# Silu in place of Sigmoid, and one product less on VectorE, in the experts of a mixture-of-experts layer on one Trainium2 core

## The chip, the cores and the metric

The kernel runs on one core of one Trainium2 chip. The metric is the time of one execution on the device in microseconds, taken over several runs; the number compared is the median. One further execution was recorded by the hardware profiler, and all rows below come from it. Engine names in rows: PE is TensorE's matmuls, PEld its weight loads, DVE is VectorE, ACT is ScalarE, POOL is GpSimd, SP is SyncE, which issues most DMA transfers here.

## The reference

One layer of a diffusion backbone over 1024 tokens of width 1024: windowed attention and a long convolution, merged and normalised, and then a mixture of 32 experts of which each token uses four. The change lies in the experts alone:

```python
hb = x_pad[tok] @ w1[e] + b1[e]
glu, lin = jnp.split(hb.astype(jnp.float32), 2, axis=-1)
glu = jnp.minimum(glu, SWIGLU_LIMIT)                      # 7.0
lin = jnp.clip(lin, -SWIGLU_LIMIT, SWIGLU_LIMIT)
act = (glu * jax.nn.sigmoid(SWIGLU_ALPHA * glu) * (lin + 1.0)).astype(h.dtype)   # alpha 1.702
yb = (act @ w2[e] + b2[e]).astype(jnp.float32)
```

With silu(z) = z·sigmoid(z), glu·sigmoid(1.702·glu) is silu(1.702·glu)/1.702.

## The kernel before

The first thousand microseconds are the attention, the convolution, the merge and the router. From about 1044 us to 2400 us the 32 experts run, and the last 50 us are the final normalisation.

**Experts.** Each expert has a fixed capacity of token rows (416 for the fullest, down to 32). Two experts are in work at any time, one in lane 0 (the large ones, fullest first) and one in lane 1 (the small ones, emptiest first); a planned list says which lane takes its next step. An expert has eight steps: four of gate and linear columns (two weight blocks each) and four of the output (one block each). A weight block of 1 MB comes from memory by an SP transfer into one of five `raw` buffers (L304). ScalarE rounds it to half precision, `wh` (L314, a Copy with a scale), and VectorE makes the remainder, `wl` (L316); both go in two halves, so that there are 768 of each. When VectorE has made `wl`, the `raw` buffer is free and SP can start the next transfer. TensorE then multiplies in three passes, high by high, high by low and low by high (L346; the smallest experts, of up to 56 rows, L343).

**The gated activation.** For each pair of gate and linear blocks VectorE adds the bias and clamps both from PSUM into SBUF (L392 `sg` and L393 `sl`; for the smallest experts L390 and L395), ScalarE computes the sigmoid of `sg` into `ss` (L396), VectorE multiplies `sg` by `ss` (L397) and then clamps `sl` from below and multiplies it by that product (L398). ScalarE rounds the result to half precision (`ah`, L402) and VectorE makes the remainder (`al`, L403). `ss` has one buffer for each lane, `sg` and `sl` two. `gpool` is false, so that the product runs on VectorE. The values are carried times 64, and L402 and L403 scale them back by 2^-8.

**Tokens in and out.** For each chunk of up to 128 rows of an expert to come, a matmul with a one-hot matrix `S` gives the row numbers (L261, cast to the index `gi` in L263), a GpSimd gather fetches the rows (`g`, L276), TensorE transposes them (L285) and ScalarE copies them to `xT` (L286). At an expert's end TensorE transposes the output, ScalarE scales it into `yr` (L435, two buffers) and a GpSimd scatter-add writes it to memory (`accD`, L436). Gathers and scatter-adds share GpSimd's one queue, in program order.

**Order.** The code is written step by step, but a scheduler that simulates the program's time line places the instructions of each engine. An edit of one operation can therefore move others.

Of the kernel before, what the change touches and what calls it, by code (L numbers as in the profile page):

```python
# [18 lines left out]
AF = mybir.ActivationFunctionType  # L19
ALU = mybir.AluOpType  # L20
# [51 lines left out]
def pecost(C): return (0.192*(mmc(2*C)+mmc(C)) if C<=CCAT else 0.576*mmc(C))+2.0*-(-C//128)  # L72
def dmacost(C): return DMAC+2.1*-(-C//128)
def plan():


    k=sum(map(dmacost,CAPS))/sum(map(pecost,CAPS))
    Q=[r for r in range(NE) if r not in HOLD]; H=list(HOLD); cur=[None,None]; out=[]; pe=PE0; dma=0.0; last=None
    while True:
        for l in range(2):  # L80
            if cur[l] is None and Q and (l==0 or CAPS[Q[-1]]<=LMAX): cur[l]=(Q.pop(0 if l==0 else -1),0)
            elif cur[l] is None and l==1 and H and (len(Q)<=HQ): cur[l]=(H.pop(0),0)
        if cur[0] is None and cur[1] is None: return out
        l=0 if pe<=dma+SLACK else 1
        if cur[l] is not None and last==l and cur[l][1]==4: l=1-l
        if cur[l] is None: l=1-l
        r,u=cur[l]; f=1/6. if u<4 else 1/12.
        pe+=pecost(CAPS[r])*k*f; dma+=dmacost(CAPS[r])*f
        out.append((l,r,u)); last=l
        cur[l]=(r,u+1) if u<7 else None  # L90
PLAN=plan()
PMAX=[max(CAPS[r] for l,r,u in PLAN if l==k) for k in range(2)]
assert sorted((r,u) for l,r,u in PLAN)==[(r,u) for r in range(NE) for u in range(8)]
class Moe:
# [144 lines left out]
    def prep_(s,C,p,pos,M,res,G0=None,late=None):  # L239
# [6 lines left out]
        def hot(i):  # L246
            c0=i*128; cs=min(128,C-c0)
            if late is not None and i>1:
                if i==2: st['w']=wk.tile([128,2,D],F16,name="g1",bufs=2).rearrange("p a (t c) -> p (a t) c",t=4)
                S=st['w'][:,:,(i-2)*128:(i-2)*128+cs]  # L250
            else: S=wk.tile([128,NT,128],F16,name="S%d"%p,bufs=min(2,-(-PMAX[p]//128)))[:,:,:cs]
            st[i]=S
# [25 lines left out]
        def tr(i):  # L278

            if i==0:  # L280
                st['x']=wk.tile([128,2,8,PMAX[p]],F16,name="xT%d"%p,bufs=1); res.append((st['x'],chunks))
            c0=i*128; cs=min(128,C-c0); g=G.pop(i)
# [73 lines left out]
    def expert_(s,C,p,reg,xT,chunks):  # L356
        nc,wk,ps,A=s.nc,s.wk,s.ps,s.A
        e=reg()
        T=lambda dt,name,bufs: wk.tile([128,PMAX[p]],dt,name=name+str(p),bufs=bufs)[:,:C]
        br=s.brs.pop(reg,None)  # L360
        if br is None: br=s.bias_load(e)
        pb=ps.tile([128,512],F32,name="tp",bufs=2)[:,:24]
        nc.tensor.transpose(pb,br,s.idf[:24,:24])
        bc=wk.tile([128,24],F32,name="bc",bufs=4)
        nc.vector.tensor_scalar(bc[:,0:8],pb[:,0:8],64.0,None,op0=ALU.mult)
        nc.vector.tensor_scalar(bc[:,8:16],pb[:,8:16],64.0,64.0,op0=ALU.mult,op1=ALU.add)
        nc.vector.tensor_tensor(bc[:,16:24],pb[:,16:24],s.g2c,op=ALU.mult)
        cat=C<=CCAT
        x=[xT[:,:,k,:C] for k in range(8)] if cat else [[xT[:,q,k,:C] for k in range(8)] for q in range(2)]
        ah,al=[],[]  # L370
        for u in range(4):

            wg=s.jget(); wl=s.jget()
            nb=2 if C<=256 else 1
            for c0 in range(0,2,nb):
                if cat:
                    t=ps.tile([128,4,2,64],F32,name="acc",bufs=4); pg,pl=t[:,0:2,:,:C],t[:,2:4,:,:C]
                elif C<=128:
                    t=ps.tile([128,4,128],F32,name="acc",bufs=4); pg,pl=t[:,0:2,:C],t[:,2:4,:C]
                else:  # L380
                    pg=ps.tile([128,nb,512//nb],F32,name="acc",bufs=4)[:,:,:C]; pl=ps.tile([128,nb,512//nb],F32,name="acc",bufs=4)[:,:,:C]
                for j in range(nb): s.mm3(pg[:,j],wg,c0+j,x,C)
                for j in range(nb): s.mm3(pl[:,j],wl,c0+j,x,C)
                if c0+nb==2: s.jahead(s.ahead)
                T2=lambda dt,name,bufs: wk.tile([128,max(2*PMAX[p],4*CCAT) if PMAX[p]<=256 else 512],dt,name=name+str(p),bufs=bufs)[:,:nb*C].rearrange("p (j c) -> p j c",j=nb)
                g=T2(F32,"sg",2); l=T2(F32,"sl",2); sg=T2(F32,"ss",1)
                for j in range(nb):
                    f=u*2+c0+j
                    if cat:
                        nc.vector.tensor_scalar(g[:,j],pg[:,j,0],bc[:,f:f+1],None,op0=ALU.add); nc.vector.tensor_scalar(l[:,j],pl[:,j,0],bc[:,8+f:9+f],None,op0=ALU.add)  # L390
                        continue
                    nc.vector.tensor_scalar(g[:,j],pg[:,j],bc[:,f:f+1],448.0,op0=ALU.add,op1=ALU.min)  # L392
                    nc.vector.tensor_scalar(l[:,j],pl[:,j],bc[:,8+f:9+f],512.0,op0=ALU.add,op1=ALU.min)  # L393
                if cat:
                    nc.vector.tensor_tensor(g,g,pg[:,:,1],op=ALU.add); nc.vector.tensor_scalar(g,g,448.0,None,op0=ALU.min); nc.vector.tensor_tensor(l,l,pl[:,:,1],op=ALU.add); nc.vector.tensor_scalar(l,l,512.0,None,op0=ALU.min)  # L395
                nc.scalar.activation(sg,g,AF.Sigmoid,scale=1.702/64)  # L396
                (nc.gpsimd if s.gpool else nc.vector).tensor_tensor(g,g,sg,op=ALU.mult)  # L397
                nc.vector.scalar_tensor_tensor(l,l,-384.0,g,op0=ALU.max,op1=ALU.mult)  # L398
                if cat:
                    hl=wk.tile([128,max(2*min(PMAX[p],256),4*CCAT)],F16,name="ah%d"%p,bufs=s.nact(p,nb))[:,:4*C].rearrange("p (j q c) -> p j q c",j=2,q=2); h,lo=hl[:,:,0],hl[:,:,1]  # L400
                else: h=T2(F16,"ah",s.nact(p,nb)); lo=T2(F16,"al",s.nact(p,nb))
                nc.scalar.activation(h,l,AF.Copy,scale=2.**-8)  # L402
                nc.vector.scalar_tensor_tensor(lo,l,2.**-8,h,op0=ALU.mult,op1=ALU.subtract)  # L403
                for j in range(nb):
                    if cat: ah.append(hl[:,j])
                    else: ah.append(h[:,j]); al.append(lo[:,j])
            yield
        yT=[]
        for u in range(4):

            w=s.jget()
            for c in range(2):
                m=u*2+c
                py=ps.tile([128,512],F32,name="acc",bufs=4)
                py=py[:,:2*C].rearrange("p (q c) -> p q c",q=2) if cat else py[:,:C]
                s.mm3(py,w,c,ah if cat else (ah,al),C)
                if c==1: s.jahead(s.ahead)
                y=T(F32,"yT",8)
                if cat:
                    nc.vector.tensor_copy(y,py[:,0]); nc.vector.tensor_tensor(y,y,py[:,1],op=ALU.add); py=y  # L420
                nc.scalar.activation(y,py,AF.Identity,bias=bc[:,16+m:17+m],scale=s.g2s[:,m:m+1])  # L421
                yT.append(y)
            yield
        s.tail.append(s.rows_out(C,chunks,yT))
        yield
# [12 lines left out]
    def experts(s,only=None):  # L438
        P=PLAN[:only]
        s.regs={}; W={}; J=[]  # L440
# [928 lines left out]
```

## Time and profile before

| | |
|---|---|
| time, median of 3 runs | 2435.37 us (2434.03 to 2435.98) |
| the profiled execution's own time | 2453.07 us |
| its span, first to last instruction | 2451.2 us |
| mean granted TensorE clock | 0.936 of full speed |
| TensorE matmuls busy | 2210.8 us, 90% of the span |
| VectorE busy | 2100.5 us, 86% |
| ScalarE busy | 1402.3 us, 57% |
| GpSimd busy | 281.9 us, 12% |

The profiled execution took 17.7 us (0.7%) longer than the median of the runs; stretches and durations are read from it, and the forecast is made for the median. Shares of busy time are means over stages with different limits, so that the experts' stage has to be read by itself.

### The profile page before, as it was taken

To read this page: it belongs to the slowest core of one execution; us is meant where nothing else is said; L and a number is where in the kernel's file an instruction comes from. 1 tells how busy PE (TensorE), PEld (TensorE's weight loads), DVE (VectorE), ACT (ScalarE), POOL (GpSimd) and SP (SyncE) were. 2 spreads that over 40 slices of the span, in tenths; PEclk is the share of its full clock that TensorE was granted. 3 is DMA by queue.
4 is the path that set the end of the run, shared out by engine and by line. 5 is a ranking of instruction groups with operands and counts; after the bars stand their busy time and mean duration, and the time that the engine had idled before them with its cause. 6 is when DMAs were issued, how large, how long until landed. Compare 5 with 4: busy or idle time off the path is not lost.

```text
span 2451.2 us, 59715 instructions
## 1 busy us (share of the span) xinstructions
PE 2210.8 (90%) x24732; PEld 1669.0 (68%) x24753; DVE 2100.5 (86%) x3907; ACT 1402.3 (57%) x2069; POOL 281.9 (12%) x176
## 2 busy tenths in 40 slices
PE   6899989999899999398998999998989999999991
PEld 4565464554544444355566678898989999999991
DVE  6767899798769759789889988998989999999995
ACT  3422334221345412457767767787867878788881
POOL 0000011000000000001021111321041111221110
PEclk9899999999779999689898989999989999999996
DMA  8425644554414332479899989999999999999984
GB/s 287 136 93 181 198 136 138 161 184 159 94 38 148 100 118 104 167 254 304 303 293 313 308 272 339 319 340 325 343 320 348 337 349 335 357 351 353 350 284 157
DMA packets 520012, 594.18 MB, mean 242 GB/s; under 512 B 16708, under 2 KB 472332, under 8 KB 519350
## 3 DMA queue, kind: packets, MB, share of 16 engines
q1 hardware_dynamic: 493048, 508.27, 61.8%
q0 software_dynamic: 13152, 43.69, 6.9%
q10 hardware_dynamic: 13534, 38.35, 4.6%
q8 instruction: 196, 3.21, 0.5%
q14 instruction: 82, 0.67, 0.1%
HBM read 532.95 MB, written 57.29 MB: 241 GB/s over the span
## 4 chain that ended last, share of the span: by engine, by line
PE 59%; DVE 23%; DMA 7%; issue 5%; ACT 3%; SPq 2%; POOL 0%; DVEq 0%; ACTq 0%; POOLq 0%
PE acc L346 30%; PE mm L812 8%; DVE wl L316 8%; PE mm L1080 3%; PE mm L1121 3%; DVE bf L722 3%; PE ff L704 2%; PE acc L343 2%; DMA g<-rows,gi 1%; PE mm L975 1%; DMA accD<-yr,si 1%; ACT wh L314 1%; PE yt L433 1%; PE ff L899 1%; DVE sl L393 1%
## 5 line engine op out<-in xcount | busy, mean ns | idle before, releaser
L316 DVE SCALAR_TENSOR_TENSOR wl<-raw,wh 128x1024 f16<-128x1024 f32 x768 | 910.2, 1216 | 62.1 <-ACT wh L314 59.0
L314 ACT ACTIVATE wh<-raw 128x1024 f16<-128x1024 f32 x768 | 768.1, 1049 | 185.9 <-PE acc L346 80.7
L346 PEld LDWEIGHTS <-wh 128*128 128x128 f16 x9984 | 785.8, 99 | 97.5 <-issue 21.8
L346 PE MATMUL acc<-xT,wh 128*128 128x80 f16 (+18 forms) x6656 | 716.9, 235 | 4.8 <-DVE yT L420 2.2
L346 PE MATMUL acc<-xT,wl 128*128 128x112 f16 (+19 forms) x3328 | 638.0, 235 | 0.0
L346 PEld LDWEIGHTS <-wl 128*128 128x128 f16 x4992 | 493.0, 99 | 46.6 <-issue 10.5
L346 PE MATMUL acc<-ah,wh 128*128 128x112 f16 (+19 forms) x1664 | 331.1, 239 | 14.7 <-ACT ah L402 6.8
L346 PE MATMUL acc<-al,wh 128*128 128x112 f16 (+19 forms) x1664 | 331.9, 240 | 6.6 <-DVE al L403 6.5
L346 PE MATMUL acc<-ah,wl 128*128 128x112 f16 (+19 forms) x1664 | 331.4, 240 | 0.0
L812 PE MATMUL mm<-hx,wh 128*128 128x512 f16 (+1 forms) x1072 | 322.4, 378 | 6.2 <-DVE hx L635 4.6
L812 PE MATMUL mm<-hx,wl 128*128 128x512 f16 x536 | 202.6, 378 | 0.0
L436 POOL DMA_INDIRECT accD<-yr,si x49 | 125.3, 2557 | 668.3 <-ACT yr L435 437.6
L812 PEld LDWEIGHTS <-wh 128*128 128x128 f16 x1072 | 105.0, 98 | 118.4 <-issue 2.3
L276 POOL DMA_INDIRECT g<-rows,gi x44 | 124.2, 2823 | 459.0 <-DVE tf L265 415.6
L722 DVE TENSOR_TENSOR bf<-bf 128x256 f32<-128x256 f32 (+1 forms) x272 | 131.2, 541 | 0.3
L421 ACT ACTIVATE yT<-acc,bc,g2s 128x112 f32<-128x112 f32 (+19 forms) x208 | 97.7, 481 | 28.2 <-PE acc L346 25.6
L812 PEld LDWEIGHTS <-wl 128*128 128x128 f16 x536 | 52.4, 98 | 65.2 <-issue 7.0
L402 ACT ACTIVATE ah<-sl 128x64 f16<-128x64 f32 (+18 forms) x140 | 56.6, 409 | 55.9 <-DVE sl L398 55.6
L343 PEld LDWEIGHTS <-wl 128*128 128x128 f16 x1152 | 79.4, 99 | 12.6 <-issue 11.2
L343 PEld LDWEIGHTS <-wh 128*128 128x128 f16 x1152 | 81.2, 104 | 6.9 <-DVE yT L420 5.2
L393 DVE TENSOR_SCALAR sl<-acc,bc 128x112 f32<-128x112 f32 (+19 forms) x208 | 75.2, 377 | 11.2 <-PE acc L346 10.8
L392 DVE TENSOR_SCALAR sg<-acc,bc 128x112 f32<-128x112 f32 (+19 forms) x208 | 75.3, 378 | 9.2 <-PE acc L346 8.6
(380 smaller groups left out, 3436.1 us busy)
## 6 DMA issues: line engine op xcount, KB each, us to landing
raw<-in_exp_w SPq DMA_DIRECT2D x384, 1024.0 KB
wr<-in_w_in SPq DMA_DIRECT2D x34, 512.0 KB
t<-in_w_mod ACTq DMA_DIRECT2D x32, 512.0 KB
bf<-in_dec SPq DMA_DIRECT2D x32, 256.0 KB
Hd<-bf ACTq DMA_DIRECT2D x32, 256.0 KB
bf<-Hd SPq DMA_DIRECT2D x32, 256.0 KB
Gd<-t ACTq DMA_DIRECT2D x16, 512.0 KB
gt<-Gd SPq DMA_DIRECT2D x32, 256.0 KB
```

The lines of the kernel that those rows point to most:

```text
L276: nc.gpsimd.indirect_dma_start(out=g[:cs].rearrange("p a d -> p (a d)"),out_offset=None,in_=s.rows,in_offset=bass.IndirectOffsetOnAxis(ap= ...
L314: else: nc.scalar.activation(wh[:,o],raw[:,o],AF.Copy,scale=sc)
L316: else: nc.vector.scalar_tensor_tensor(wl[:,o],raw[:,o],64.0,wh[:,o],op0=ALU.mult,op1=ALU.subtract)
L343: nc.tensor.matmul(ps_,wh,x[k],start=k==0,stop=False); nc.tensor.matmul(ps_[:,0],wl,x[k][:,0],start=False,stop=k==7)
L346: nc.tensor.matmul(ps_,a,b,start=n==0,stop=n==23); n+=1
L392: nc.vector.tensor_scalar(g[:,j],pg[:,j],bc[:,f:f+1],448.0,op0=ALU.add,op1=ALU.min)
L393: nc.vector.tensor_scalar(l[:,j],pl[:,j],bc[:,8+f:9+f],512.0,op0=ALU.add,op1=ALU.min)
L421: nc.scalar.activation(y,py,AF.Identity,bias=bc[:,16+m:17+m],scale=s.g2s[:,m:m+1])
L436: st=nc.gpsimd.indirect_dma_start(out=s.accD,out_offset=bass.IndirectOffsetOnAxis(ap=si[:cs,:1],axis=0),in_=yr[:cs],in_offset=None,compute ...
L722: (nc.gpsimd if pool and s.usepool else nc.vector).tensor_tensor(o,a,b,op=op)
L812: nc.tensor.matmul(p,w[a][:,k,:],s.hx[b][:,k,o],start=i==0,stop=i==23); i+=1
L1080: nc.tensor.matmul(p,w[a_][:,k,m*128:(m+1)*128],X[x][:,k,o] if b==0 else X[x][:,k,:],start=n==0,stop=n==11); n+=1
```

## The change

ScalarE's activation is Silu instead of Sigmoid, of the same input with the same scale 1.702/64 into the same buffer `ss`. The product L397 is gone, and the clamp-and-multiply reads `ss` instead of `sg`. Since silu(1.702·glu) is 1.702 times what the product gave, divided by 64, the scale of the two last instructions becomes 0.25/1.702 in place of 2^-8.

```diff
 PLAN=plan()
+HSC=0.25/1.702
...
-                nc.scalar.activation(sg,g,AF.Sigmoid,scale=1.702/64)
-                (nc.gpsimd if s.gpool else nc.vector).tensor_tensor(g,g,sg,op=ALU.mult)
-                nc.vector.scalar_tensor_tensor(l,l,-384.0,g,op0=ALU.max,op1=ALU.mult)
+                nc.scalar.activation(sg,g,AF.Silu,scale=1.702/64)
+                nc.vector.scalar_tensor_tensor(l,l,-384.0,sg,op0=ALU.max,op1=ALU.mult)
...
-                nc.scalar.activation(h,l,AF.Copy,scale=2.**-8)
-                nc.vector.scalar_tensor_tensor(lo,l,2.**-8,h,op0=ALU.mult,op1=ALU.subtract)
+                nc.scalar.activation(h,l,AF.Copy,scale=HSC)
+                nc.vector.scalar_tensor_tensor(lo,l,HSC,h,op0=ALU.mult,op1=ALU.subtract)
```

In the code the Python names `g`, `l` and `sg` stand for the tiles `sg`, `sl` and `ss`. One line is added at the top, so that lines 92 to 396 of the kernel before are 93 to 397 in the changed one; from L398 on the numbers agree again.

On VectorE, the first gated activation of the first expert (capacity 416) stands like this before:

```order
L392 TENSOR_SCALAR sg_10389<-acc,bc 128x416
L397 TENSOR_TENSOR sg_10389<-sg_10389,ss_10391 128x416
L393 TENSOR_SCALAR sl_10390<-acc,bc 128x416
L398 SCALAR_TENSOR_TENSOR sl_10390<-sl_10390,sg_10389 128x416
L403 SCALAR_TENSOR_TENSOR al_10398<-sl_10390,ah_10397 128x416
L392 TENSOR_SCALAR sg_10467<-acc,bc 128x416
L316 SCALAR_TENSOR_TENSOR wl<-raw,wh 128x1024 x2
L397 TENSOR_TENSOR sg_10467<-sg_10467,ss_10469 128x416
L393 TENSOR_SCALAR sl_10468<-acc,bc 128x416
```

and like this now:

```order
L393 TENSOR_SCALAR sg_10389<-acc,bc 128x416
L394 TENSOR_SCALAR sl_10390<-acc,bc 128x416
L398 SCALAR_TENSOR_TENSOR sl_10390<-sl_10390,ss_10391 128x416
L403 SCALAR_TENSOR_TENSOR al_10397<-sl_10390,ah_10396 128x416
L393 TENSOR_SCALAR sg_10466<-acc,bc 128x416
L317 SCALAR_TENSOR_TENSOR wl<-raw,wh 128x1024 x2
L394 TENSOR_SCALAR sl_10467<-acc,bc 128x416
```

The product is gone from between the two clamps, and the instruction that frees `ss` is now L398.

On ScalarE, the same place begins like this before (the table load there is the last one ahead of the final normalisation, in both programs):

```order
L396 ACT_TABLE_LOAD
L396 ACTIVATE ss_10391<-sg_10389 128x416
L402 ACTIVATE ah_10397<-sl_10390 128x416
L314 ACTIVATE wh<-raw 128x1024 x2
L396 ACTIVATE ss_10469<-sg_10467 128x416
L314 ACTIVATE wh<-raw 128x1024 x4
L402 ACTIVATE ah_10475<-sl_10468 128x416
```

and now:

```order
L397 ACT_TABLE_LOAD
L397 ACTIVATE ss_10391<-sg_10389 128x416
L402 ACTIVATE ah_10396<-sl_10390 128x416
L315 ACTIVATE wh<-raw 128x1024 x2
L397 ACTIVATE ss_10468<-sg_10466 128x416
L315 ACTIVATE wh<-raw 128x1024 x4
L402 ACTIVATE ah_10473<-sl_10467 128x416
```

Nothing moved here: one table load, at the same place, and the copies of the weights between two activations need no load of their own.

On GpSimd's queue, the gathers and scatter-adds around the end of the expert of capacity 384 stand as follows. The scatter-adds are, in this order, one of a small expert, three of the 384-row expert's chunks and one of another small expert; the gathers of 56, 64 and 72 rows are for lane-1 experts to come, those of 128 rows for lane 0. Before:

```order
L276 DMA g_15038<-rows,gi 56x2048
L436 DMA accD<-yr,si 1152x1024 x4
L276 DMA g_16122<-rows,gi 64x2048
L436 DMA accD<-yr,si 1152x1024
L276 DMA g_16481<-rows,gi 128x2048
L276 DMA g_16861<-rows,gi 128x2048
L276 DMA g_17306<-rows,gi 72x2048
```

and now:

```order
L277 DMA g_15004<-rows,gi 56x2048
L436 DMA accD<-yr,si 1152x1024
L277 DMA g_16082<-rows,gi 64x2048
L277 DMA g_16437<-rows,gi 128x2048
L436 DMA accD<-yr,si 1152x1024 x4
L277 DMA g_16815<-rows,gi 128x2048
L277 DMA g_17256<-rows,gi 72x2048
```

The gathers of 64 rows and of the first 128 rows moved ahead of the scatter-adds of the 384-row expert. Six other gathers of the stage stand behind one to three more scatter-adds than before, among them one of 88 rows behind three more; all the rest stand as they stood.

## Rows read from the trace of the kernel before

**Rows 1.** The page's first part: engine, busy us, share, count.

```profile
PE 2210.8 (90%) x24732; PEld 1669.0 (68%) x24753; DVE 2100.5 (86%) x3907; ACT 1402.3 (57%) x2069; POOL 281.9 (12%) x176
```

**Rows 2.** Two stretches: length; PE, PEld, DVE, ACT, POOL busy; clock; DMA share, GB/s.

```profile
1050.00:1700.00 650.00, 592.70 (x7942) 467.05 (x7940) 592.54 (x1178) 471.14 (x662) 123.89 (x44) 0.93 0.94 307
1700.00:2400.00 700.00, 679.41 (x10831) 671.33 (x10831) 650.55 (x1037) 565.23 (x770) 122.74 (x47) 0.97 1.01 333
```

**Rows 3.** The chain that ended last, by line, in the same two stretches.

```profile
by line: PE acc L346 39.0%; DVE wl L316 18.0%; issue 8.4%; PE acc L343 6.3%; DMA accD<-yr,si 3.7%; DMA g<-rows,gi 3.2%; ACT wh L314 2.9%; DVE sl L393 2.1%; DVE sg L392 1.7%; DVE S L253 1.7%; DVE sg L397 1.4%; DVE sl L398 1.4%; DVE al L403 1
by line: PE acc L346 66.5%; DVE wl L316 11.6%; issue 3.9%; PE yt L433 3.0%; DMA g<-rows,gi 3.0%; DVE sl L393 1.7%; DVE sg L392 1.6%; DMA raw<-in_exp_w 1.6%; PE tp L285 1.4%; DVE sg L397 1.1%; DVE sl L398 1.0%; ACT wh L314 1.0%; DVE al L403 
```

**Rows 4.** Groups of instructions: count, busy us, mean ns, idle before, releaser.

```profile
L398 DVE SCALAR_TENSOR_TENSOR sl<-sl,sg 128x64 f32<-128x64 f32 (+18 forms) x140 | 57.9, 415 | 0.7
L397 DVE TENSOR_TENSOR sg<-sg,ss 128x64 f32<-128x64 f32 (+18 forms) x140 | 57.7, 415 | 1.7 <-ACT ss L396 1.5
L396 ACT ACTIVATE ss<-sg 128x64 f32<-128x64 f32 (+18 forms) x140 | 56.7, 408 | 42.1 <-DVE sg L392 36.3 <-DVE sg L395 4.4 <-DVE sg L397 0.9
L402 ACT ACTIVATE ah<-sl 128x64 f16<-128x64 f32 (+18 forms) x140 | 56.6, 409 | 55.9 <-DVE sl L398 55.6
```

**Rows 5.** Waits, 1050 to 2400 us: total us, times, longest.

```profile
ACT ah L402 <- DVE sl L398: 55.6, 40, 5.9
DVE wl L316 <- ACT wh L314: 46.7, 59, 5.0
```

**Rows 6.** Waits of SP's DMA queue in the same stretch.

```profile
SPq L304 <- DVE wl L316: 604.1, 213, 11.4
```

**Rows 7.** ScalarE's groups by form: another activation, and the table load.

```profile
L830 ACT ACTIVATE t<-mm,cb,cwm 128x512 f32<-128x512 f32 x16 | 12.4, 774 | 0.0
...
L396 ACT ACT_TABLE_LOAD x1 | 1.3, 1283 | 0.0
```

**Rows 8.** Groups over the whole span: ScalarE's Sigmoid of the merge gates.

```profile
L841 ACT ACTIVATE t<-mm 128x512 f32<-128x512 f32 x32 | 18.9, 589 | 51.2 <-PE mm L812 51.2
```

**Rows 9.** GpSimd in order of time: start us, us, idle before, releaser.

```profile
1374.06 3.37 POOL L436 DMA_INDIRECT accD<-yr,si  x1 [44.55 <-ACT yr L435]
...
1396.10 2.02 POOL L436 DMA_INDIRECT accD<-yr,si  x1 [8.43 <-issue]
1398.42 1.56 POOL L276 DMA_INDIRECT g<-rows,gi  x1 [0.30 <-issue]
...
1626.85 1.63 POOL L276 DMA_INDIRECT g<-rows,gi  x1 [37.50 <-DVE tf L265]
...
1660.26 2.44 POOL L436 DMA_INDIRECT accD<-yr,si  x1 [8.24 <-DMA accD<-yr,si]
```

**Rows 10.** VectorE in order of time: the index of the 64-row gather.

```profile
1391.92 0.14 DVE L263 CAST gi<-tp 64x1 int32<-64x1 f32 x1
```

**Rows 11.** TensorE in order of time: the transposes of those 64 rows.

```profile
1407.11 0.60 PE L285 MATMUL tp<-idh,g 64*128 64x64 f16 x8 [5.90 <-DMA g<-rows,gi]
```

**Rows 12.** Busy time in three stretches around that wait; columns as in rows 2.

```profile
1400.00:1405.00 5.00, 1.21 (x14) 0.87 (x12) 5.00 (x13) 3.26 (x5) 0.00 (x0) 1.00 1.08 296
1405.00:1410.00 5.00, 2.89 (x18) 1.86 (x19) 3.98 (x7) 0.00 (x0) 3.53 (x1) 0.56 1.07 348
1410.00:1415.00 5.00, 5.00 (x68) 3.79 (x66) 1.73 (x5) 1.81 (x2) 1.22 (x2) 0.76 1.09 353
```

**Rows 13.** ScalarE in order of time: the copies of the gathered 88 rows.

```profile
1686.71 1.38 ACT L286 ACTIVATE xT<-tp 128x704 f16<-128x704 f16 x2
```

**Rows 14.** All engines in order of time: two activations of lane 1 (capacity 112).

```profile
1922.85 0.39 ACT L396 ACTIVATE ss<-sg 128x224 f32<-128x224 f32 x1
1925.21 0.38 DVE L397 TENSOR_TENSOR sg<-sg,ss 128x224 f32<-128x224 f32 x1
1927.32 0.38 ACT L396 ACTIVATE ss<-sg 128x224 f32<-128x224 f32 x1
1928.75 0.38 DVE L398 SCALAR_TENSOR_TENSOR sl<-sl,sg 128x224 f32<-128x224 f32 x1
```

## The prediction, made blind

> **What bounds the kernel now.** I read the busy times first, then the stage in stretches, then the chain that ended last, then the waits. Over the span TensorE is busiest and VectorE second [rows 1]; the experts' stage has to be read by itself. In its first 650 us no engine is full: TensorE 592.7 us and VectorE 592.5 us busy, so that each idles for 57 us, at a granted clock of 0.93. In the last 700 us TensorE is busy for 679.4 us, VectorE for 650.6 us, and the DMA engines have a share of 1.01 [rows 2]. TensorE thus has 57.3 us of idle time to give back in the first stretch and 20.6 us in the second.
>
> The chain says who sets the pace. It runs through TensorE's expert matmuls for 39.0% of the first stretch and 66.5% of the second, and through VectorE's `wl` for 18.0% and 11.6%; the product L397, which the change removes, is on it for 1.4% and 1.1% [rows 3]. VectorE is not the one bound, but it is on the path again and again: it does its instructions in order, a ready weight block waits behind the gated activation, and SP's queue waits for `wl` before it can fill the next `raw` buffer, 213 times for 604.1 us in all [rows 6]. ScalarE waits 40 times, 55.6 us, for L398 before it can make `ah`, with the next `wh` behind it in its queue, and VectorE waits 46.7 us for `wh` [rows 5].
>
> **The change part by part.**
>
> *The product goes.* 140 instructions of 415 ns, 57.7 us of VectorE's time [rows 4]. Most of that lies beside TensorE's work. On the path lie 1.4% of 650 us, 9.1 us, and 1.1% of 700 us, 7.7 us [rows 3]. The first I count in full, since TensorE has 57 us to give there. The second I halve to 3.9 us: where TensorE is busy for 97% of the time, what leaves VectorE's part of the path is soon found again on TensorE's. Sum 13.0 us. From both sides: nothing, if other work fills each gap, and 57.7 us, if VectorE's busy time were the path throughout. I stay with the row that names the path.
>
> *Silu for Sigmoid.* Silu is nowhere in the trace. Sigmoid took 408 ns in the mean, a Copy of the same sizes 409 ns [rows 4]: two functions, one price. The dearest activation near it is one of 128x512 with a scale and a bias from tiles, 774 ns, against 589 ns for a Sigmoid of that size [rows 7, 8], 31% more. So the bounds are 0 and 0.31 × 56.7 = 18 us of ScalarE's time, spread over 140 instructions. ScalarE idles for 1350 − 1036 = 314 us in the stage [rows 2], and its input and operands stay the same, so I take 0. Were ScalarE's idle time gone, those 18 us would come back in full and the gain would be lost.
>
> *L398 reads `ss`, L402 and L403 take another constant.* The same instructions with the same sizes: 0. The cover that is lost is the early release of `ss`: L397 freed it, now L398 does, several instructions later on VectorE. That is the slower rival below. In the other direction `ah` comes sooner: of the 55.6 us that ScalarE waits for L398 [rows 5], 40 waits can each shorten by one L397, 0.4 us, which is 17 us of ScalarE's idle time; it is 0 in the sum, since what it moves on the path is already in the 13.0 us.
>
> *The queue of GpSimd.* The scheduler has moved instructions. The place that matters is the 64-row gather. Its index was ready at 1391.92 [rows 10], but it stood behind the scatter-adds of the 384-row expert, the last of which began at 1396.10, so that it went out at 1398.42 [rows 9]. TensorE waited 5.90 us for it [rows 11], and then ran at a granted clock of 0.56 and 0.76 for 5 us each, which costs 0.44 × 5 + 0.24 × 5 = 3.4 us more [rows 12]. In the changed order the gather is ahead of these scatter-adds, and with a free queue it could go out 6.5 us earlier, more than the wait. Price 0 to 9.3 us. VectorE was busy in all of the 5 us in which TensorE waited [rows 12], so part of the wait would be found again behind it: I take two thirds, 6 us. Of the gathers that now stand behind more scatter-adds, the 88-row one went out at 1626.85; behind the third scatter-add, which began at 1660.26 and took 2.44, it would go at 1662.7 [rows 9]. Its rows are copied only at 1686.71 [rows 13], 24 us later, and the 64-row gather needed 1407.11 − 1398.42 = 8.7 us: covered, 0. Without that cover it would cost a wait like the one above.
>
> The sum is 13.0 + 6 = 19 us. It is made against the profiled execution, which took 17.7 us longer than the median; scaled by 0.7% it stays 19 us. Forecast: 2435.4 − 19 = 2416 us.
>
> **A rule that speaks against it.** For all 140 Sigmoids, with Copies of the weights between them, the trace has one table load, of 1283 ns [rows 4, 7]. The Trainium skill, in "ScalarE: Activation LUTs", section "Table sets: the hidden batching unit", says that functions are loaded in named sets, that a switch to another set is paid each time, and that kernels should batch activations by set. Its list does not show which set holds Silu. The trace agrees as far as it goes: the Copies between the Sigmoids needed no load. What the rule would cost here, were Silu and Copy not in one set, is the last rival.
>
> **The rivals.** *TensorE and the transfers set the pace (no room).* The last 700 us speak for it: 97% busy, DMA share 1.01 [rows 2]. Then the second stretch gives nothing, half of the 9.1 us of the first is found again on TensorE, and the moved gather's time goes behind VectorE: 4.6 us, 2431 us. Against it: SP's queue waits for VectorE, not the other way round [rows 6], and 57 us of TensorE's idle time in the first stretch.
>
> *VectorE is the bound more than the chain says.* Each instruction that leaves its queue brings every later `wl` and transfer forward, on the path or not. At most its own time is gained, in the first stretch half of 57.7 us, 29 us, in the second half of TensorE's 20.6 us, 10 us, and 6 us for the gather: 45 us, 2390 us. For it: VectorE at 91% to 93% [rows 2]. Against it: L397's small share of the chain [rows 3].
>
> *`ss` is held too long (slower).* Lane 1's Silu at 1927.32 would meet a buffer that L398 frees only at 1929.13; before, L397 had freed it at 1925.59 [rows 14]. Brought forward by one L397 that is a wait of 1.81 − 0.38 = 1.43 us, with `wh` blocked behind it on ScalarE. It becomes slower than now by more than 0.2% (about what a measurement of this kernel can tell from no change, 4.9 us) when such waits on the path exceed 19 + 4.9 us: 17 of the 140. With 30 of them, 43 us against 19, the time is 2459 us. Against it: ScalarE's idle time, and only one wait for L397 now, of 0.9 us [rows 4].
>
> *A load at each Silu (it does not do what it says).* If Silu and the Copies between needed different tables, each of 140 Silus would pay two loads, 140 × 2 × 1.283 = 359 us of ScalarE's time [rows 7], which exceeds its 314 us of idle time: up to 2794 us. The changed program has one load at the old place and none between the copies, so this is all but excluded.
>
> **How the numbers follow.** The forecast has 0.69, "no room" 0.13, VectorE's bound 0.10, the held buffer 0.07, the loads 0.01. The forecast's own range is 2402 (all of the chain's 16.8 us, the gather's 9.3 us and 7 of the 17 us of ScalarE's shorter waits) to 2428 (half of the 13.0 us, and 1 us for the gather). From 2396 to 2431 it also holds "no room" and part of the third case, and leaves out the two slower cases and the far end of VectorE's. Faster by over 0.2%: 0.66 of the forecast, 0.10, and 0.06 of "no room", 0.82. Within 0.2%: the rest of those two, 0.10. Slower: 0.08.
>
> **What would show it.** L397's group is gone and VectorE's busy time is near 2043 us; Silu's mean is near 408 ns, with one load. The 5.90 us wait of the transposes at 64 rows is gone, and the 64-row gather stands ahead of the 384-row scatter-adds. ScalarE's wait for L398 ahead of `ah` is below 55.6 us. TensorE's idle time shrinks more in the first stretch than in the last 700 us. Wrong would be: a wait of Silu for L398 of tens of us, new gather waits ahead of the transposes, or a Silu mean well over 408 ns.

## The result, and the profile after

The changed kernel takes 2401.5 us (median of 4 runs, 2394.4 to 2412.7) against 2435.7 us for the kernel before (4 runs, 2434.0 to 2444.2): a ratio of 0.9846, with a 95% interval from 0.981 to 0.9881. That is 34 us less where 19 were forecast, between the forecast (2416) and the rival in which VectorE is the bound (2390). The time lies inside the stated range of 2396 to 2431, but just below 2402, the lower end of the range that was the forecast's own: it lies in the part that was kept for that rival.

The profiled executions differ by a little more: 2412.69 us after, 2453.07 before, 11 and 17 us above their medians. The first part of the page of the changed kernel answers to [rows 1].

```profile
span 2410.9 us, 59658 instructions
PE 2199.2 (91%) x24732; PEld 1659.4 (69%) x24753; DVE 2053.8 (85%) x3767; ACT 1399.8 (58%) x2069; POOL 287.6 (12%) x176
```

VectorE has 140 instructions and 46.7 us of work fewer. TensorE does the same 24732 matmuls in 11.6 us less. As the span is 40.3 us shorter, TensorE idles for 28.7 us less.

The stage in two stretches, columns as in [rows 2]. The second ends at 2350 us here, since the changed kernel is through with the experts soon after.

```profile
1050.00:1700.00 650.00, 611.20 (x8383) 486.11 (x8382) 589.21 (x1128) 491.45 (x691) 131.06 (x45) 0.96 0.97 320
1700.00:2350.00 650.00, 637.44 (x10293) 630.52 (x10292) 606.60 (x946) 539.16 (x734) 120.63 (x46) 0.99 1.05 347
```

The same second stretch of the kernel before, and its chain by line there:

```profile
1700.00:2350.00 650.00, 629.95 (x10051) 622.28 (x10052) 612.94 (x985) 527.93 (x717) 117.11 (x44) 0.97 1.04 342
...
by line: PE acc L346 64.6%; DVE wl L316 12.4%; issue 4.3%; DMA g<-rows,gi 3.2%; PE yt L433 2.7%; DVE sl L393 1.8%; DVE sg L392 1.7%; DMA raw<-in_exp_w 1.7%; PE tp L285 1.5%; DVE sg L397 1.2%; DVE sl L398 1.1%; ACT wh L314 1.0%; DVE al L403 
```

In the first stretch TensorE's idle time falls from 57.3 us [rows 2] to 38.8 us, with 441 more matmuls done; in the second from 20.1 to 12.6 us, with 242 more. The granted clock rises in both, from 0.93 to 0.96 and from 0.97 to 0.99. VectorE is nearly as busy in these stretches as before, at 91% and 93%, since more of the expert work now falls into them.

The chain that ended last, by line, in the same two stretches of the changed kernel, answers to [rows 3].

```profile
by line: PE acc L347 62.8%; DVE wl L317 8.8%; PE acc L344 6.7%; issue 3.5%; ACT wh L315 3.0%; PE yt L433 2.2%; DMA g<-rows,gi 1.7%; DMA raw<-in_exp_w 1.6%; PE tp L286 1.3%; DVE S L254 0.9%; DVE yT L420 0.9%; ACT xT L287 0.7%; DVE sl L394 0.
...
by line: PE acc L347 75.7%; DVE wl L317 5.0%; DMA raw<-in_exp_w 3.5%; DMA g<-rows,gi 3.2%; PE yt L433 3.1%; issue 2.0%; PE tp L286 1.9%; ACT wh L315 1.2%; DVE sl L394 0.8%; DVE sg L393 0.6%; PE tp L262 0.6%; DVE al L403 0.5%; DVE sl L398 0.
```

This is the largest change of all. `wl` falls from 18.0% to 8.8% and from 12.4% to 5.0%, and the expert matmuls (L346, now L347) rise from 39.0% to 62.8% and from 64.6% to 75.7%. The removed product had 1.4% and 1.2%. The path lost far more than the product's own entries on it. These shares differ between executions, though: in a second profiled execution of the changed kernel (in the experiments below) `wl` has 12.5% and 7.7%. They give the direction and not a price.

Where in the stage the time was gained is told by the scatter-adds, of which both kernels have the same ones in the same order. Two of the 49 in GpSimd's time line before, the 22nd and the last:

```profile
1716.04 1.45 POOL L436 DMA_INDIRECT accD<-yr,si  x1 [19.55 <-ACT yr L435]
...
2408.18 1.32 POOL L436 DMA_INDIRECT accD<-yr,si  x1 [5.75 <-DMA accD<-yr,si]
```

and after:

```profile
1689.79 1.50 POOL L436 DMA_INDIRECT accD<-yr,si  x1 [19.57 <-ACT yr L435]
...
2367.58 1.31 POOL L436 DMA_INDIRECT accD<-yr,si  x1 [6.57 <-DMA accD<-yr,si]
```

The 22nd starts 26.3 us sooner and the last 40.6 us. The experts' stage itself began 4.3 us later in this execution (its table load starts at 1048.66 instead of 1044.37). So the first stretch gave about 31 us and the rest about 14 us, where the forecast had 15 and 4. The second execution of the changed kernel gives 32 and 16 in the same way (1033.13, 1672.74 and 2349.30). The sums, 45 and 48 us, belong to single executions; the medians differ by 34.

The groups of the gated activation in the changed kernel, to be held against [rows 4], and the only table load in the experts' stage, from the view by form:

```profile
L398 DVE SCALAR_TENSOR_TENSOR sl<-sl,ss 128x64 f32<-128x64 f32 (+18 forms) x140 | 58.1, 416 | 2.7
L397 ACT ACTIVATE ss<-sg 128x64 f32<-128x64 f32 (+18 forms) x140 | 56.8, 408 | 38.2 <-DVE sg L393 32.7 <-DVE sg L396 4.2 <-issue 0.5
L402 ACT ACTIVATE ah<-sl 128x64 f16<-128x64 f32 (+18 forms) x140 | 56.5, 407 | 33.2 <-DVE sl L398 32.8
...
L397 ACT ACT_TABLE_LOAD x1 | 1.3, 1283 | 0.0
```

Silu takes 408 ns, what Sigmoid took, with one load. No wait of Silu (L397) for L398 is among its releasers: the longer hold of `ss` costs no wait. The waits of the changed kernel in the stage (total us, times, longest) answer to [rows 5]:

```profile
DVE wl L317 <- ACT wh L315: 40.6, 54, 10.1
...
ACT ah L402 <- DVE sl L398: 32.8, 23, 4.7
ACT ss L397 <- DVE sg L393: 32.7, 17, 7.6
ACT wh L315 <- DMA raw<-in_exp_w: 28.1, 30, 2.3
```

ScalarE waits for L398 for 32.8 us instead of 55.6.

### The profile page after: what moved, and what is told of

The parts are those of the page before. It is cut to its first block, busy times and chain, and to the rows that moved or that the text cites. A ratio compares the mean times of both kernels' runs of the same rounds, so it can differ in the third digit from the quotient of the medians.

```text
span 2410.9 us, 59658 instructions
## 1 busy us (share of the span) xinstructions
PE 2199.2 (91%) x24732; PEld 1659.4 (69%) x24753; DVE 2053.8 (85%) x3767; ACT 1399.8 (58%) x2069; POOL 287.6 (12%) x176
## 4 chain that ended last, share of the span: by engine, by line
PE 72%; DVE 15%; DMA 6%; ACT 3%; issue 3%; SPq 1%; DVEq 0%; ACTq 0%; POOLq 0%
PE acc L347 38%; PE mm L812 10%; DVE wl L317 4%; PE mm L1080 4%; PE mm L1121 3%; DVE bf L722 2%; PE ff L704 2%; DMA raw<-in_exp_w 2%; PE acc L344 2%; PE mm L975 2%; PE yt L433 1%; ACT wh L315 1%; DMA g<-rows,gi 1%; PE ff L899 1%; PE mm L572 1%
## 5 line engine op out<-in xcount | busy, mean ns | idle before, releaser
L315 ACT ACTIVATE wh<-raw 128x1024 f16<-128x1024 f32 x768 | 769.9, 1050 | 181.7 <-PE acc L347 92.6
L347 PEld LDWEIGHTS <-wh 128*128 128x128 f16 x9984 | 778.2, 99 | 85.8 <-issue 12.9
L347 PE MATMUL acc<-xT,wh 128*128 128x80 f16 (+18 forms) x6656 | 717.3, 235 | 2.9 <-ACT wh L315 1.2
L347 PE MATMUL acc<-xT,wl 128*128 128x112 f16 (+19 forms) x3328 | 638.0, 235 | 2.3 <-DVE wl L317 2.3
L347 PEld LDWEIGHTS <-wl 128*128 128x128 f16 x4992 | 488.9, 98 | 45.7 <-issue 7.2
L347 PE MATMUL acc<-ah,wh 128*128 128x112 f16 (+19 forms) x1664 | 323.9, 236 | 6.0 <-ACT yT L421 3.0
L347 PE MATMUL acc<-al,wh 128*128 128x112 f16 (+19 forms) x1664 | 323.3, 236 | 3.7 <-DVE al L403 3.7
L347 PE MATMUL acc<-ah,wl 128*128 128x112 f16 (+19 forms) x1664 | 322.3, 236 | 0.0
L277 POOL DMA_INDIRECT g<-rows,gi x44 | 139.2, 3165 | 459.5 <-DVE tf L266 435.4
L436 POOL DMA_INDIRECT accD<-yr,si x49 | 115.9, 2366 | 617.2 <-ACT yr L435 383.3
L393 DVE TENSOR_SCALAR sg<-acc,bc 128x112 f32<-128x112 f32 (+19 forms) x208 | 75.3, 377 | 12.4 <-PE acc L347 12.2
L791 ACT ACTIVATE wh<-wr 128x1024 f16<-128x1024 f32 (+1 forms) x49 | 38.4, 813 | 72.0 <-PE mm L812 51.7
```

Of the source, the lines that this page charges most:

```text
L277: nc.gpsimd.indirect_dma_start(out=g[:cs].rearrange("p a d -> p (a d)"),out_offset=None,in_=s.rows,in_offset=bass.IndirectOffsetOnAxis(ap= ...
L315: else: nc.scalar.activation(wh[:,o],raw[:,o],AF.Copy,scale=sc)
L347: nc.tensor.matmul(ps_,a,b,start=n==0,stop=n==23); n+=1
L436: st=nc.gpsimd.indirect_dma_start(out=s.accD,out_offset=bass.IndirectOffsetOnAxis(ap=si[:cs,:1],axis=0),in_=yr[:cs],in_offset=None,compute ...
```

## The experiments

Three causes were to be told apart: VectorE's freed time, whatever the order; the shorter chain of dependent steps from the gate to `ah` (one instruction less between Silu and L398); and the new order in GpSimd's queue, which brought the 64-row gather forward. Next to them stood the price of Silu and the hold of `ss`. Ratios are to the kernel before on the same chip, with 95% intervals. Where no other base is named, the edit is one of the changed kernel. The expected times are laid out from a kernel before at 2435.7 us; beside these runs it took 2440.5 to 2444.8 us. So ratios are compared, and a time that missed what was expected is named.

**Sigmoid again, without the product.**

```diff
-                nc.scalar.activation(sg,g,AF.Silu,scale=1.702/64)
+                nc.scalar.activation(sg,g,AF.Sigmoid,scale=1.702/64)
```

> The changed kernel with Sigmoid in Silu's place, still without the product (so that the gated value itself is left out of the result). If Silu costs what Sigmoid costs, the program runs as the changed one does: 2401 us within 10 us, and the activation's mean is 408 ns in both. If Silu were dearer, this one would be faster than the changed kernel by up to 18 us.

Measured: 0.9822 [0.9786, 0.9857], the changed kernel's ratio within the intervals. Its activation took 408 ns in the mean as well. Silu costs what Sigmoid does, and the gain does not come from it.

**The product put back, with nobody to read it.** The added line stands behind the Silu; the chain from gate to `ah` stays as short as in the changed kernel, and VectorE gets back its 140 instructions.

```diff
                 nc.scalar.activation(sg,g,AF.Silu,scale=1.702/64)
+                nc.vector.tensor_tensor(g,g,sg,op=ALU.mult)
```

> The changed kernel with VectorE's product of gate and activation put back where it stood, its result read by nobody: VectorE's 57.7 us are back, but the clamp-and-multiply needs only the Silu. If VectorE's time is what was gained, the time goes back to 2425 to 2440 us. If the shorter chain of dependences from the activation to the rounded value is what was gained, it stays near 2400 to 2410 us.

Measured: 1.0023 [0.999, 1.0056]. All of the gain is gone (2448.5 us, above the 2425 to 2440 expected for this case). The page's first part, the stage from 1050 to 2350 us, one of its waits, the chain by line there, and the group of the 64-row transposes:

```profile
PE 2213.4 (90%) x24752; PEld 1669.4 (68%) x24753; DVE 2098.4 (86%) x3907; ACT 1403.3 (57%) x2069; POOL 298.0 (12%) x176
```

```profile
1050.00:2350.00 1300.00, 1221.20 (x18013) 1087.21 (x18012) 1202.48 (x2161) 1000.11 (x1377) 254.55 (x88) 0.96 0.99 326
```

```profile
ACT ah L403 <- DVE sl L399: 59.2, 35, 4.7
```

```profile
by line: PE acc L347 43.6%; DVE wl L317 18.8%; issue 5.8%; DMA g<-rows,gi 4.0%; PE acc L344 2.6%; DMA raw<-in_exp_w 2.6%; DVE sl L394 2.3%; DVE sg L393 2.1%; PE yt L434 2.0%; DVE sl L399 1.4%; DVE al L404 1.4%; ACT wh L315 1.2%; DVE sg L398
```

```profile
L286 PE MATMUL tp<-idh,g 64*128 64x64 f16 x32 | 1.4, 191 | 0.0
```

Three things follow. The dependent steps are as few as in the changed kernel, yet nothing is gained: their number is not the cause. `wl` is on the chain for 18.8% of these 1300 us, in the changed kernel's two executions for 6.9% and 10.1%, and ScalarE waits for L398 (here L399) for 59.2 us, against 55.6 before [rows 5] and 32.8 in the changed kernel: that wait is one for VectorE's queue, not for the product itself. And in this kernel the 64-row gather still stands ahead of the scatter-adds of the 384-row expert, with no wait left at those transposes (0.0 us in the last row), without a gain: with 0.999 as the interval's lower end, the new order brings at most 2.4 us in this kernel, not the 6 us that the forecast gave it. TensorE's waits for gathers are 17.3 us in all here, against 18.1 us before; they come up at other experts.

**Silu in place, no `ss`.**

```diff
-                g=T2(F32,"sg",2); l=T2(F32,"sl",2); sg=T2(F32,"ss",1)
+                g=T2(F32,"sg",2); l=T2(F32,"sl",2)
...
-                nc.scalar.activation(sg,g,AF.Silu,scale=1.702/64)
-                nc.vector.scalar_tensor_tensor(l,l,-384.0,sg,op0=ALU.max,op1=ALU.mult)
+                nc.scalar.activation(g,g,AF.Silu,scale=1.702/64)
+                nc.vector.scalar_tensor_tensor(l,l,-384.0,g,op0=ALU.max,op1=ALU.mult)
```

> The changed kernel with Silu written in place over the clamped gate, which has two buffers for each lane, so that the single buffer is no longer held until the clamp-and-multiply. If the held buffer costs something, this is faster than the changed kernel by 3 to 15 us. If ScalarE's waits for it lie beside other work, it is within 10 us of 2401 us, the scatter of a new order.

Measured: 0.9817 [0.9781, 0.9852], with the changed kernel's ratio inside the interval. The single buffer of `ss` costs nothing that can be measured.

**The kernel before, with its product on GpSimd.** This frees VectorE by the other way, but puts the product into a slower engine's queue.

```diff
-    NG=2; hact=True; pools=True; ahead,gpool,rhp=2,False,1000
+    NG=2; hact=True; pools=True; ahead,gpool,rhp=2,True,1000
```

> The kernel before with the product on GpSimd: VectorE is relieved of the same 57.7 us, but the chain of dependences is as long as before or longer, and GpSimd's queue of gathers gets 140 more instructions. If VectorE's time alone counts, 2395 to 2415 us. If the chain's length or GpSimd's queue counts, slower than that: 2420 to 2460 us.

Measured: 1.0063 [1.0037, 1.0089], slower. Its busy times and its groups, by line:

```profile
PE 2207.3 (90%) x24752; PEld 1670.3 (68%) x24753; DVE 2082.8 (85%) x3767; ACT 1400.3 (57%) x2069; POOL 507.3 (21%) x316
...
L316 DVE SCALAR_TENSOR_TENSOR wl<-raw,wh 128x1024 f16<-128x1024 f32 x768 | 923.2, 1238 | 43.8 <-ACT wh L314 42.3 <-PE acc L346 0.3
...
L397 POOL TENSOR_TENSOR sg<-sg,ss 128x64 f32<-128x64 f32 (+18 forms) x140 | 252.2, 1817 | 448.5 <-ACT ss L396 444.3 <-DMA accD<-yr,si 3.8
...
L398 DVE SCALAR_TENSOR_TENSOR sl<-sl,sg 128x64 f32<-128x64 f32 (+18 forms) x140 | 66.1, 474 | 61.6 <-POOL sg L397 59.7
```

One product takes 1817 ns there against 415 ns [rows 4], and VectorE waits 59.7 us for it with L398 at the head of its queue, more than the 57.7 us of the product's own records. Its busy time falls by only 17.7 us, from 2100.5 to 2082.8, as `wl` takes 13.0 us more in all and L398 8.2 us more. So this run says nothing against VectorE's time as the cause: the time was not freed.

**The old order of the gathers.** The gather of 64 rows is held behind the scatter-adds of the 384-row expert, and that of the first 128 rows of the 256-row expert behind the next one too, as in the kernel before; the product stays out. The gathers that the changed order holds back stay where it put them.

```diff
+            b={(64,0):(384,256),(256,0):(48,0)}.get((C,i))
+            with (s.tc.issue_after(s.scat[b].ins) if b else ExitStack()):
...
-            st=nc.gpsimd.indirect_dma_start(out=s.accD,...
+            s.scat[(C,c0)]=st=nc.gpsimd.indirect_dma_start(out=s.accD,...
```

> The changed kernel with the gathers of 64 and 128 rows queued again behind the scatter-adds of the 384-row expert, as in the kernel before. If their new place is worth the 6 us of the prediction (0 to 9 us), the time is 2404 to 2411 us. If VectorE's relief is nearly all of the gain, it stays within 5 us of the changed kernel's 2400 us.

Measured: 0.9852 [0.9819, 0.9886], with the changed kernel's ratio inside the interval. GpSimd's time line shows the gather behind the third of these scatter-adds, 10.5 us sooner by the clock than in the kernel before [rows 9], as all that stands ahead of it is:

```profile
1385.30 2.34 POOL L438 DMA_INDIRECT accD<-yr,si  x1 [8.62 <-DMA accD<-yr,si]
1387.95 0.97 POOL L279 DMA_INDIRECT g<-rows,gi  x1 [0.30 <-issue]
```

No cost of the old order is seen. But 6 us are 0.0025 of the time, less than the half-width of this interval, and the time of 2406.9 us lies where 6 us were expected to put it (2404 to 2411), with the kernel before 4.8 us slower beside it: this run alone neither shows the 6 us nor excludes them. What speaks against them is the unread product, in which the new order brings no gain.

**Half of the product, and the product twice.** The unread product in every second step (70 instructions), and two of them in every step (280):

```diff
+                if u%2==0: nc.vector.tensor_tensor(g,g,sg,op=ALU.mult)
```

> The unread product of VectorE is put back in every second gated activation only: 70 of 140, 29 us. If the time goes with VectorE's time, it lies half way between the changed kernel and the one with all 140 products, 2415 to 2425 us. If only a threshold matters (VectorE full or not), it is near one of the two, 2400 or 2440 us.

```diff
+                nc.vector.tensor_tensor(g,g,sg,op=ALU.mult)
+                nc.vector.tensor_tensor(g,g,sg,op=ALU.mult)
```

> The unread product is put back twice: 280 instructions, 115 us of VectorE. If VectorE's queue sets the pace and each us of its time costs 0.6 to 0.9 us, the time is 2460 to 2495 us, as far above the kernel before as the changed one is below it. If the gain came from the scheduler's order, there is no reason for a second step of that size, and it stays at 2435 to 2455 us.

Measured: 0.987 [0.9833, 0.9907] with half, 1.0135 [1.0098, 1.0172] with two. With half, the 2412.5 us lie between the two cases that were expected, much nearer to the changed kernel: half of the product out of VectorE's queue already brings most of the gain. A second one put in costs about as much again as the gain. TensorE and VectorE in the stage with two products, and in the changed kernel, from 1050 to 2350 us:

```profile
1050.00:2350.00 1300.00, 1205.82 (x17685) 1077.24 (x17683) 1225.27 (x2261) 983.67 (x1351) 271.81 (x88) 0.94 0.97 319
```

```profile
1050.00:2350.00 1300.00, 1248.64 (x18674) 1116.62 (x18673) 1195.81 (x2073) 1030.61 (x1424) 251.69 (x91) 0.98 1.01 333
```

With two products in every step, VectorE's share of this stretch rises from 92.0% only to 94.3%, but TensorE gets 989 matmuls fewer done in it, at a granted clock of 0.94 instead of 0.98.

**Less still for VectorE.** If VectorE's time went on being the price, more relief would bring more. In the first kernel ScalarE reads the matmul's result from PSUM itself, adds the biases and applies Silu and Relu, for all but the smallest experts; the Relu's bias is chosen so that Relu is the linear half's lower clamp. VectorE clamps that half from above, caps the Silu at `SMAX`, its value at the gate's limit, and multiplies. In the second kernel only Silu reads from PSUM, and the gate's upper clamp is left out.

```diff
-                    nc.vector.tensor_scalar(g[:,j],pg[:,j],bc[:,f:f+1],448.0,op0=ALU.add,op1=ALU.min)
-                    nc.vector.tensor_scalar(l[:,j],pl[:,j],bc[:,8+f:9+f],512.0,op0=ALU.add,op1=ALU.min)
+                    nc.scalar.activation(sg[:,j],pg[:,j],AF.Silu,bias=bc[:,f:f+1],scale=1.702/64)
+                    nc.scalar.activation(l[:,j],pl[:,j],AF.Relu,bias=bc[:,8+f:9+f])
...
+                    nc.vector.tensor_scalar(l,l,896.0,-384.0,op0=ALU.min,op1=ALU.add)
+                    nc.vector.scalar_tensor_tensor(l,sg,SMAX,l,op0=ALU.min,op1=ALU.mult)
```

> For experts of more than 56 rows ScalarE takes both halves straight from PSUM with their biases, Silu for the gate and Relu for the linear half, and VectorE clamps behind it: VectorE has one instruction less for each of 208 blocks' halves, some 50 to 75 us less, and ScalarE some 75 to 90 us more. If VectorE is still on the path and ScalarE has room, 2375 to 2395 us. If TensorE or the transfers now set the pace, 2395 to 2405 us. If ScalarE becomes the one that is waited for, slower: 2405 to 2440 us.

```diff
-                    nc.vector.tensor_scalar(g[:,j],pg[:,j],bc[:,f:f+1],448.0,op0=ALU.add,op1=ALU.min)
+                    nc.scalar.activation(sg[:,j],pg[:,j],AF.Silu,bias=bc[:,f:f+1],scale=1.702/64)
```

> For experts of more than 56 rows ScalarE's Silu reads the gate half straight from PSUM with its bias; the upper clamp of the gate half is left out, the linear half stays on VectorE as in the changed kernel. VectorE has 208 instructions of 377 ns less, some 75 us, and ScalarE only the price of 68 more instructions and the PSUM reads, 20 us. If VectorE's time still sets the pace, 2365 to 2385 us. If TensorE and the weight transfers now do, 2385 to 2400 us: the further gain is less than half of what the first 57.7 us gave.

The first took 2388.6 us, inside the range expected if more relief goes on paying, but its ratio is 0.9814 with a wide interval, 0.9744 to 0.9885; the second 0.9857 [0.9819, 0.9896], with 2404.0 us above both ranges expected for it. So the changed kernel and the first of these were run once more.

> The changed kernel itself once more, beside the next one on the same chip: 2395 to 2412 us, 1.3% to 1.9% below the kernel before.

> The kernel in which ScalarE reads both halves from PSUM once more, in more rounds. If VectorE's further relief is worth something, its ratio to the kernel before lies below the changed kernel's by 0.004 or more, with intervals apart. If ScalarE's added work takes it back, the two agree within 0.003.

Measured: the changed kernel 0.9844 [0.9816, 0.9871], the other 0.9816 [0.9782, 0.985]. Its estimate is below that of the changed kernel both times, by some 7 us, but the intervals overlap, and the 0.0028 of the second pair count, just, as agreement by what was expected: whether it is a little faster stays open. What is plain is that 54 us of VectorE's time less (the gate without a clamp), and even 88 us less with 70 us more on ScalarE, bring little or nothing. Two waits of the kernel with the gate alone read from PSUM, and one of the other's second run:

```profile
DVE wl L317 <- ACT wh L315: 81.5, 97, 3.8
ACT wh L315 <- DMA raw<-in_exp_w: 47.3, 43, 3.3
```

```profile
DVE wl L317 <- ACT wh L315: 129.3, 130, 4.4
```

In the changed kernel these two waits were 40.6 and 28.1 us. VectorE, freed further, waits longer for ScalarE's `wh`, and in the first of these kernels ScalarE waits longer for the weights.

## Why the forecast came out too small

The kernels with more or less work for VectorE, by its busy time over the span, with two figures of the profiled executions: the matmuls that TensorE got done from 1050 to 2350 us, and the length of the experts' stage, from its table load to the start of its last scatter-add. The stage begins between 1028 and 1049 us, by 15 us apart even in the two executions of the changed kernel; that shifts the matmuls of a fixed stretch, and the stage's length is free of it.

| kernel | VectorE busy, us | ratio, 95% interval | matmuls | stage, us |
|---|---|---|---|---|
| product twice | 2142.8 | 1.0135 [1.0098, 1.0172] | 17685 | 1391.2 |
| before | 2100.5 | 1 | 17993 | 1363.8 |
| product once, unread | 2098.4 | 1.0023 [0.999, 1.0056] | 18013 | 1360.0 |
| product in every second step | 2075.1 | 0.987 [0.9833, 0.9907] | 18506 | 1330.2 |
| the change | 2053.8 | 0.9846 [0.981, 0.9881] | 18674 | 1318.9 |
| the change again | 2052.8 | 0.9844 [0.9816, 0.9871] | 18722 | 1316.2 |
| gate from PSUM, no clamp | 2000.0 | 0.9857 [0.9819, 0.9896] | 18745 | 1319.4 |
| gate and linear half by ScalarE | 1965.6 | 0.9814 [0.9744, 0.9885] | 18641 | 1308.9 |
| gate and linear half by ScalarE, again | 1965.8 | 0.9816 [0.9782, 0.985] | 18782 | 1312.0 |

**The failed step is the price of the product, 13.0 us.** The forecast took the product's own entries on the chain, 9.1 us and half of 7.7 us. Putting the product back alone costs (1.0023 − 0.9846) × 2435.7 = 43 us, by the ends of the two intervals 27 to 60 us. The chain names the instruction that was last at each point. VectorE works its queue in order and is busy for over 90% of the stage: the next `wl` is late by what stood ahead of it, the products among it, and is itself the entry. From 1050 to 2350 us, `wl` has 19.9% of the chain with two products, 15.2% before, 18.8% with the unread one, 13.6% with half, 6.9% and 10.1% in the two executions of the change, and 5.2% in the last kernel of the table. That it is through `wl` that the product delays the path is argued from these shares; that the product's time on VectorE is what costs is shown by putting it back.

One row had said so, and the forecast weighed it too lightly: 91% to 93% of VectorE [rows 2]. SP's waiting for `wl` [rows 6] speaks less plainly, since after the change SP still waits for it 202 times, 539.4 us in all:

```profile
SPq L305 <- DVE wl L317: 539.4, 202, 11.3
```

**What the product takes from VectorE** was also read too high. The 57.7 us add up 140 records, and VectorE's records overlap: the product of [rows 14] is recorded for 0.38 us from 1925.21, but the next instruction starts 0.30 us after it:

```profile
1925.51 0.33 DVE L392 TENSOR_SCALAR sg<-acc,bc 128x112 f32<-128x112 f32 x1
```

VectorE's busy time, in which overlaps count once, fell by 46.7 us, and rose by 44.6 us with the unread product. So the bound of 57.7 us was out of reach, and "near 2043 us" came out at 2053.8. Against these 46.7 us, 34 to 43 us gained are most of them.

**The form of the gain.** From two products to half of one, 68 us of VectorE's busy time bring (1.0135 − 0.987) × 2435.7 = 65 us: a microsecond of VectorE is worth about one. From half of the product to none, 21 us bring 6 us by the ratios and 11 to 14 us by the stages, and the next 53 to 88 us little or nothing. That the gain levels off is shown; that it does so within the change rests on the one kernel with half. A straight line from two products to none would put that kernel at 0.9915, some 11 us above its 0.987 and outside its interval, but programs that take the same work from VectorE differ by up to 8.5 us among themselves (0.9817 in place, 0.9852 with the old order of the gathers): each edit makes the scheduler place instructions anew. For the same reason the step from the single product to half of it, 37 us for 23, need not be steeper than one. So the rival "VectorE is the bound" was right on the mechanism, and "no room" on what follows behind the bend. That the time still lay in the stated range is in part luck: a price too low by some 20 to 30 us stood beside 6 us for a gather for which no run shows a gain.

**Halving the last stretch** was wrong too. It gave 14 to 16 us in the profiled executions, not 3.9. The forecast reasoned that TensorE at 97% had no room; but at a lower clock the same matmuls keep it busy for longer, and where the gaps became shorter the granted clock stood higher, 0.99 there instead of 0.97. Over the whole span TensorE's busy time for the same matmuls is 11.6 us less, a term that the sum did not have. That the shorter gaps raised the clock is argued; no run changed the gaps alone.

**The gather, 6 us,** is not seen in any run: the unread product has the new order without a gain, and the old order costs nothing that its interval could tell. The 3.4 us that it priced the clock at were also too many: they count in 2.1 us of [rows 12] in which TensorE did nothing. As the prediction asked, the 5.90 us wait is gone and the gather stands ahead; but another came, which the prediction had named as a sign of being wrong: the transposes of 96 rows, with 2.1 us before, wait 7.07 us after.

```profile
1677.48 1.46 PE L286 MATMUL tp<-idh,g 96*128 96x96 f16 x16 [7.07 <-DMA g<-rows,gi]
```

TensorE's waits for gathers fall from 18.1 us in all to 10.2. In the kernel with the old order they are 5.8 us: they do not follow from this one place in the queue. The 88-row gather was covered, as forecast, and shows no wait.

**What held:** Silu at no price, with one load (so the rival of a load at each Silu falls); L398 with another source at 416 ns; no wait for `ss`, neither in the trace nor by the kernel without it, so that the slower rival falls; TensorE's idle time shrinking more in the first stretch (18.5 us) than in the last (7.5). ScalarE's wait for L398 shrank, by 22.8 us, but not because L398 has one step less to wait for: with the unread product it has as few, and the wait is 59.2 us. VectorE is less behind. That "no room" would leave 4.6 us is refuted.

**What stays open** is what sets the pace behind the bend. TensorE is busy for 1248.6 of 1300 us there, and the transfers move 333 GB/s both in the changed kernel and, with 88 us less of VectorE's work, in the last one; the traces speak for both, and no run here slowed or relieved either of them alone.

## What to carry to other kernels

In this kernel the share of one line on the chain that ended last lay far below its price, on an engine that works in order and is over 90% busy (16.8 us of entries, 34 us gained). There the chain's share is a low estimate and the time that the line takes from the engine, with overlaps counted once (46.7 us here), a high one; what the next engine can take caps the gain. Putting the removed instruction back, unread, tells an engine's time from a chain of dependent steps in one run, and half of it or double shows how the gain runs. A stall at one place that another order would remove should not be counted as a gain while a fuller engine stands behind it.

## What the runs showed of the hardware

With the product on GpSimd, one takes 1817 ns in the mean where VectorE took 415 ns, 4.4 times as long. That mean is no fixed price: products of one size took between 0.32 and 4.75 us there.

```profile
1263.08 4.75 POOL L397 TENSOR_TENSOR sg<-sg,ss 128x64 f32<-128x64 f32 x1 [2.53 <-ACT ss L396]
...
1286.26 0.32 POOL L397 TENSOR_TENSOR sg<-sg,ss 128x64 f32<-128x64 f32 x1 [0.48 <-ACT ss L396]
```

In that kernel VectorE's own L398 took 474 ns instead of 415, and `wl` 1238 ns instead of 1216. The two engines run side by side there, but what slows either wasn't tried by itself.
